# Seven products for eight: the second product onto a copy of the first, and a unit's last two behind the next unit's first

## The chip, the core and the metric

The kernel runs on one core of a Trainium2 chip. The metric is the device time of one execution in microseconds, as the median of several runs. The engines are called by the short names of the profile: PE (TensorE, the matrix engine; PEld is its weight load), DVE (VectorE), ACT (ScalarE), POOL (GpSimd) and SP (SyncE, which issues the DMAs). PE writes only into PSUM, so every product must be copied or added out of PSUM by DVE or ACT. That step is called an eviction here.

## The reference

One inference step of one layer of a streaming encoder with three gated branches, over 1024 prompt tokens and 64 sample tokens, in float32:

```
shift, scale, gate = silu(c) @ W_ada + b_ada
h = rmsnorm(x, pre_g) * (1 + scale) + shift
z = h @ w_in                      # 1024 x 8720, cut into the branches' columns
A: trailing means minus token, per-group linear;  B: spatial gating on chunks of 128
C: gated linear attention with a low-rank decay
y_a, y_b, y_c: each branch * silu(its gate columns)
m = sigmoid(gm_a) * (y_a @ w_oa) + sigmoid(gm_b) * (y_b @ w_ob) + sigmoid(gm_c) * (y_c @ w_oc)
out = m @ w_out
y = x + gate * rmsnorm(out, post_g)
```

Outputs are y for both token sets, the pooling history, the attention state and the normalised rows of branch B.

## The kernel before

Every float32 operand is split into two parts, `hi` and `lo` (function `split`, L359, for activations and `w_split`, L555, for weights), and a product is the sum of hi·hi, hi·lo and lo·hi. The large projections go through `s_unit` (L573). One unit makes 256 output channels for all tokens: the two halves of its channels, the even and odd blocks of 128 input channels, and the two token pieces of 544 (512 prompt and 32 sample) form a 2 x 2 block product, which Winograd's form does with seven products instead of eight. There are 42 units: 34 for w_in, with four input blocks per product (`nkk` = 4, 24 matmuls of 272 columns), four for w_oa with two blocks (12 matmuls) and four for w_oc with four.

A unit holds three PSUM tiles of two banks each: `pA` and `pB`, which it takes in turn from two (`spsum`, L212), and `pC`, the tile `third` (L207). In the profile the first two are called `sps` and the last `third`. The order of one unit (L618 to L663), with what is evicted behind each product:

1. B11 into pA; ACT copies it to `p1`.
2. T2 into pB; DVE: `u2 = p1 + pB`.
3. B21 onto pA; ACT copies it to `c11`, which is finished.
4. T3 onto pB; DVE: `u3 = p1 + pB`.
5. T1 into pC; DVE: `u3 += pC`.
6. T4 onto pB; DVE: `p1 += pB`, finished.
7. B22 onto pC; DVE: `u2 += pC`; `u2` and `u3` are finished.

A product that goes onto a tile must wait for the eviction of what stands there. The names that count for the profile are `u<-p,sps` (steps 2 and 4), `u<-u,third` (steps 5 and 7), `p<-p,sps` (step 6), `p<-sps` (step 1) and `c<-sps` (step 3). Behind a finished tile runs `post`, which differs by unit (a tanh on ACT, a gate, transposes) and ends in a store, issued by `put_later` one step on. In the last two projections `post_m` (L1377) also loads `z_gm` and `z_m` blocks by DMA and adds them.

The first unit of each of the three operands (`feed`, L620 to L627) computes B11, T2 and T1 together, block by block, as its operands are made.

Generators set the program's order. `run` plays units one after the other and `weave` (L1729) plays the steps of a second task between those of units: the decay (L725), nine stretches of the attention (`gla`, `gla_sample`) among 19 units of w_in (L1801, L1814, L1844), the spatial gating, the loads of the next operand. Except at the very start, a planner then sets the order on each engine: it takes the program's order as priority, lets weight loads and weight splits go 400 places ahead (`ahead`), and uses its own estimate of times. On the chip each engine works through its list in that order, and an instruction that waits holds up all behind it on its engine.

The phases are: w_in units (to L1846), the w_oa units (L1874), plain products for w_ob (L1880), the w_oc units (L1893 and L1903), the last product `out_phase` (L1915).

Of the kernel before, what the change touches and what calls it, by code (L numbers as in the profile page):

```python
# [58 lines left out]
class InOrder:  # L59
    """an engine whose instructions, while asked for, keep the order of the program"""  # L60
# [18 lines left out]
def tile_hybrid_pool_sgu_gla_step(  # L79
# [55 lines left out]
    def nm(base):  # L135
        serial[0] += 1
        return f"{base}_{serial[0]}"
# [58 lines left out]
    def role(name, dt=F32):  # L196
        """a tile of the attention; each role has its own slots, so that none waits
        for a tile of another role that comes earlier in the program"""
        return roles[name](name, dt)[:, 0:TH]
# [11 lines left out]

    def spsum():  # L212
        return psum.tile([P, 2, 512], F32, name=nm("sps"), tag="sps", bufs=2)
# [4 lines left out]
    # ------------------------------------------------------------ constants  # L218
# [30 lines left out]
    def condition():  # L249
        """silu of the conditioning rows, as columns"""  # L250
        ps = apsum()
        c = cols[:, 46:62]
        pe.transpose(ps[:, 0:16], crows, ident[0:16, 0:16])
        dve.tensor_copy(c, ps[:, 0:16])
        act.activation(th_c, c, AF.Tanh, scale=0.5)
        dve.scalar_tensor_tensor(ccv, th_c, 1.0, c, op0=ALU.add, op1=ALU.mult)
        dve.tensor_scalar(
            cc[:, :, 0:2], ccv.rearrange("p (s k) -> p k s", s=2), 0.5, None, op0=ALU.mult
        )
        dve.tensor_copy(ccs[:, :, 0:2], cc[:, :, 0:2])  # L260
        dve.tensor_sub(ccs[:, :, 2:4], cc[:, :, 0:2], ccs[:, :, 0:2].bitcast(F32))
        dve.tensor_add(pair, ident[0:4, 0:2], ident[0:4, 2:4])
# [22 lines left out]
    # ------------------------------------------------------------ scratch in DRAM  # L285
# [39 lines left out]
    # ------------------------------------------------------------ x  # L325
# [63 lines left out]
    def x_transpose(k, p):  # L389
        """one half of the prompt, channels on partitions"""  # L390
# [61 lines left out]
    # ------------------------------------------------------------ adaLN  # L452
# [29 lines left out]
    def ada_shift_scale(q):  # L482
        """the shift and the scale of two k blocks"""
# [63 lines left out]
    # ------------------------------------------------------------ products, seven for eight  # L547
# [25 lines left out]
    def s_unit(src, c0, Bb, nkk, post, off=0, raw=None, feed=None):  # L573
        """256 output channels by all tokens; channels on partitions.  The two column
        halves, the even and odd k blocks and the two token pieces are the 2 x 2 blocks
        of the two operands (Winograd's form with seven products)."""
# [41 lines left out]
        pA, pB = spsum(), spsum()  # L618
        vA, vB = pA[:, :, 0:CH], pB[:, :, 0:CH]
        if feed:  # L620
            pC = third
# [5 lines left out]
            feed(nkk)  # L627
        else:
            product(pA, A(0, 0), "B11", True)
        p1 = stage("p1", F32)  # L630
        act.copy(view(p1), vA)
        yield nkk
        if not feed:
            product(pB, s2, "T2", True)
        u2 = stage("u2", F32)
        dve.tensor_add(view(u2), view(p1), vB)
        yield nkk
# [7 lines left out]
        u3 = stage("u3", F32)  # L645
        dve.tensor_add(view(u3), view(p1), vB)
        yield nkk
        if not feed:
            pC = third
            product(pC, s1, "T1", True)  # L650
        vC = pC[:, :, 0:CH]
        dve.tensor_add(view(u3), view(u3), vC)
        yield nkk
        product(pB, A(1, 1), "T4", False)
        dve.tensor_add(view(p1), view(p1), vB)
        post(1, 0, p1)
        yield nkk
        s4 = sf(A(0, 1), s2, True)
        product(pC, s4, "B22", False)
        dve.tensor_add(view(u2), view(u2), vC)  # L660
        post(0, 1, u2)
        post(1, 1, u3)
        yield nkk  # L663

    # ------------------------------------------------------------ constants used later
# [43 lines left out]
    # ------------------------------------------------------------ decay  # L709
# [15 lines left out]
    def decay(din):  # L725
# [3 lines left out]
        for terms in ((("B11", 0),), (("B21", 1),), (("T1", 0), ("B22", 1))):  # L729
            ps = third if len(acc) == 2 else spsum()  # L730
# [14 lines left out]
        d = blk("zd")[0:32, 0:PC]  # L745
        act.copy(halves(d), acc[0])
# [12 lines left out]
        def soft(items):  # L759
            """log sigmoid of each (src, dst, bias): min(x, 0) - ln(1 + exp(-|x|))"""  # L760
# [61 lines left out]
    # ------------------------------------------------------------ first phase: w_in  # L822
# [28 lines left out]
    def silu2(t):  # L851
        """t = 2 * silu(t)"""
        th = blk("th")[:, 0:PC]
        act.activation(th, t, AF.Tanh, scale=0.5)
        dve.scalar_tensor_tensor(t, th, 1.0, t, op0=ALU.add, op1=ALU.mult)
# [203 lines left out]
    # ------------------------------------------------------------ attention  # L1059
# [21 lines left out]
    def level_mask(li, s, L):  # L1081
        """the valid pairs of one level, the same for each of four chunks"""
# [3 lines left out]
    def decayed(q, k, bc, W, L):  # L1086
        """exp of the chunk totals, k scaled to the chunk's end, q scaled from its start"""
# [267 lines left out]
    def w_unit(src, c0, nk, alloc=None):  # L1355
        """hi and lo of 256 columns, as k block -> (hi, lo)"""
# [20 lines left out]
    def post_m(br, u):  # L1377
        """one branch's part of the sum; the last one's blocks go on to the last product"""
# [36 lines left out]
    def plain_units(w, src):  # L1415
        """one branch's part of the sum by plain products, onto what is there"""
# [99 lines left out]
    def wo_load(n, kks=range(4)):  # L1516
        """what is read of w_out for one of the seven products"""
# [7 lines left out]
    def wo_in(n):  # L1525
        """the moving operand of one of the seven products, a k block at a time"""
# [38 lines left out]
    def out_phase(w, sums):  # L1565
# [16 lines left out]
        def final(i, h, t, eng, n=P):  # L1582
            """one half of the columns of a token block"""
# [16 lines left out]
        def finish():  # L1600
            """the rest of the token block that was ready last, behind the next one's product"""
# [17 lines left out]
        def tail(ps, w, odd, first, last):  # L1619
            """hi and lo of the sample rows side by side, so that one product serves both"""  # L1620
# [98 lines left out]
    # ------------------------------------------------------------ order of emission  # L1719
# [9 lines left out]
    def weave(main, side, ratio):  # L1729
        """main, with so much of side in between"""  # L1730
# [10 lines left out]
        run(side)  # L1741

    with first:
# [31 lines left out]
        def feed(j):  # L1775
# [10 lines left out]
        run(s_unit(win, O_Q, Hb, 4, keep(z_q[0:2]), raw=raw, feed=feed))  # L1786
        weave(
            chain(win_unit(O_K, keep(z_k[0:2])), win_unit(O_Q + 256, keep(z_q[2:4]))),
            decay(din),
# [17 lines left out]
        for u in range(2):  # L1807
# [7 lines left out]
            chain(  # L1815
                *(
                    win_unit(o + u * 256, post(u))
                    for u in range(2)
                    for o, post in ((O_U, post_u), (O_GB, post_gb))
# [6 lines left out]
        weave(sgu(), chain(*gm[0:3]), 3.0)  # L1826
# [18 lines left out]
        run(gate_steps)  # L1845
# [20 lines left out]
    def units(w, blocks, nkk, br, us=range(4)):  # L1866
# [8 lines left out]
        units(woa, Ab, 2, 0),  # L1875
# [17 lines left out]
    run(units(woc, Cb, 4, 2, range(3)))  # L1893
# [9 lines left out]
    for n, step in zip(PRODUCTS, zip(units(woc, Cb, 4, 2, (3,)), steps)):  # L1903
# [73 lines left out]
```

## Time and profile before

| | |
|---|---|
| runs (three) | 1338.26, 1342.36, 1343.36 us |
| median | 1342.36 us |
| span of the profiled execution | 1337.9 us |
| busy PE | 92% |
| busy DVE, ACT, POOL | 71%, 42%, 50% |
| DMA | 195.38 MB, mean 146 GB/s |

The profile is of one execution. "Busy" is a share of the span; idle time of PE shows up in the list of PE's waits with the instruction that ended it. The granted clock of PE is given per stretch as a share of the full 2.4 GHz; 0.5 is the lower level of 1.2 GHz.

### The profile page before, as it was taken

The numbers are of one execution on the slowest core, as the hardware profiler recorded it, in microseconds if no ns is written. First come the engines' busy times: TensorE is split into PE (matmuls) and PEld (weight loads), VectorE is DVE, ScalarE is ACT, GpSimd is POOL, SyncE is SP. The second block draws the span as 40 slices with busy tenths as digits, with TensorE's granted clock in tenths as the row PEclk, the third lists the DMA queues.
The fourth block names the chain that finished last, engine by engine and source line by source line (L and its number), as shares of the span: only waits on it lengthen the run. The fifth ranks groups of instructions, "written<-read, shape, count | busy, mean of one in ns | idle before, by whom it ended". The sixth has DMA issues, their size and how long they took to land.

```text
span 1337.9 us, 23855 instructions
## 1 busy us (share of the span) xinstructions
PE 1226.6 (92%) x8962; PEld 1147.0 (86%) x8962; DVE 948.3 (71%) x1458; ACT 562.1 (42%) x1133; POOL 674.5 (50%) x528
## 2 busy tenths in 40 slices
PE   5789899998999998999999999899997998997796
PEld 3289799997989998999998999899987898996674
DVE  6975844556675788786468757876459789779957
ACT  7636533353534324345333345355354333233533
POOL 4652344333443546463347445253337498568625
PEclk9889899998999999999999999999998998999898
DMA  8512523232423213232235535445456799667065
GB/s 284 162 58 72 193 82 108 88 121 74 139 74 113 68 52 117 70 118 73 76 102 197 166 109 163 146 142 153 118 164 213 257 343 337 201 203 267 19 198 198
DMA packets 144609, 195.38 MB, mean 146 GB/s; under 512 B 18505, under 2 KB 82047, under 8 KB 144494
## 3 DMA queue, kind: packets, MB, share of 16 engines
q1 hardware_dynamic: 144494, 193.86, 44.5%
q8 instruction: 70, 1.15, 0.3%
q14 instruction: 45, 0.37, 0.1%
HBM read 133.59 MB, written 60.22 MB: 145 GB/s over the span
## 4 chain that ended last, share of the span: by engine, by line
PE 45%; DVE 13%; DMA 6%; issue 4%; POOL 3%; ACT 1%; SPq 0%; DVEq 0%; POOLq 0%; ACTq 0%
PE sps L70 27%; PE third L70 11%; PE aps L70 7%; DVE x L70 4%; DVE h L70 3%; DMA h<-z_m 1%; DVE u L70 1%; DMA late<-in_ada_w_dram 1%; DVE lo L70 1%; DVE late L70 1%; POOL sf L70 1%; DMA x<-z_yc 1%; DVE p L70 1%; POOL x L70 1%; DMA x<-z_bc 1%
## 5 line engine op out<-in xcount | busy, mean ns | idle before, releaser
L70 PE MATMUL sps<-h,hi 128*128 128x272 f32 x3344 | 589.1, 296 | 19.1 <-ACT x L70 6.9
L70 PEld LDWEIGHTS sps<-h,hi 128*128 128x128 f32 x3344 | 486.9, 193 | 27.9 <-ACT x L70 7.7
L70 PE MATMUL sps<-h,lo 128*128 128x272 f32 x1672 | 358.8, 295 | 2.1 <-DVE lo L70 1.9
L70 PEld LDWEIGHTS sps<-h,lo 128*128 128x128 f32 x1672 | 269.5, 192 | 5.6 <-DVE lo L70 2.8
L70 PE MATMUL third<-h,hi 128*128 128x272 f32 x1344 | 237.0, 294 | 12.4 <-DVE u L70 8.3
L70 PEld LDWEIGHTS third<-h,hi 128*128 128x128 f32 x1344 | 193.7, 190 | 16.4 <-DVE u L70 5.0
L70 ACT CAST hi<-sf 128x512 fp32r<-128x512 f32 (+1 forms) x168 | 100.3, 598 | 196.5 <-PE sps L70 160.5
L70 PE MATMUL third<-h,lo 128*128 128x272 f32 x672 | 144.3, 294 | 0.6 <-POOL lo L70 0.6
L70 ACT CAST hi<-raw 128x512 fp32r<-128x512 f32 (+1 forms) x134 | 80.1, 598 | 139.2 <-PE third L70 69.6
L70 POOL TENSOR_TENSOR lo<-sf,hi 128x512 fp32r<-128x512 f32 (+1 forms) x57 | 77.5, 1360 | 96.7 <-ACT hi L70 68.4
L70 DVE TENSOR_TENSOR lo<-sf,hi 128x512 fp32r<-128x512 f32 (+1 forms) x111 | 90.9, 819 | 42.7 <-ACT hi L70 35.7
L70 POOL TENSOR_TENSOR sf<-raw,raw 128x512 f32<-128x512 f32 (+1 forms) x38 | 50.1, 1319 | 140.3 <-DMA raw<-in_w_in_dram 71.6
L70 POOL TENSOR_TENSOR lo<-raw,hi 128x512 fp32r<-128x512 f32 (+1 forms) x45 | 61.0, 1357 | 100.6 <-ACT hi L70 88.1
L70 DVE TENSOR_TENSOR x<-x 128x256 f32<-128x256 f32 (+6 forms) x142 | 95.9, 707 | 22.2 <-DMA x<-z_bc 8.2
L70 PEld LDWEIGHTS third<-h,lo 128*128 128x128 f32 x672 | 106.8, 189 | 3.5 <-issue 1.7
L70 POOL TENSOR_TENSOR x<-x,x 128x256 f32<-128x256 f32 (+2 forms) x71 | 73.2, 1041 | 71.1 <-ACT x L70 52.4
L70 DVE TENSOR_TENSOR u<-p,sps 128x544 f32<-128x544 f32 x84 | 60.2, 717 | 63.1 <-PE sps L70 55.4
L70 ACT ACTIVATE x<-x 128x512 f32<-128x512 f32 (+2 forms) x104 | 57.9, 567 | 105.1 <-DVE x L70 96.3
L70 DVE TENSOR_TENSOR lo<-raw,hi 128x512 fp32r<-128x512 f32 (+1 forms) x89 | 77.0, 865 | 34.3 <-ACT hi L70 23.6
L70 DVE TENSOR_TENSOR u<-u,third 128x544 f32<-128x544 f32 x84 | 60.1, 716 | 47.5 <-PE third L70 47.3
L70 POOL TENSOR_TENSOR sf<-raw,sf 128x512 f32<-128x512 f32 (+1 forms) x38 | 51.5, 1356 | 78.2 <-DVE lo L70 77.4
L70 DVE TENSOR_TENSOR x<-x,x 128x256 f32<-128x256 f32 (+4 forms) x100 | 71.1, 723 | 12.9 <-ACT x L70 12.3
(290 smaller groups left out, 1918.3 us busy)
## 6 DMA issues: line engine op xcount, KB each, us to landing
raw<-in_w_in_dram SPq DMA_DIRECT2D x68, 512.0 KB, 3.9
x<-z_gm SPq DMA_DIRECT2D x48, 272.0 KB, 4.8
x<-z_m SPq DMA_DIRECT2D x32, 272.0 KB, 5.4
h<-z_m SPq DMA_DIRECT2D x28, 272.0 KB, 5.0
h<-in_x_prompt_dram SPq DMA_DIRECT2D x28, 256.0 KB, 6.1
z_gm<-u SPq DMA_DIRECT2D x24, 272.0 KB, 2.2
h<-in_ada_w_dram SPq DMA_DIRECT2D x24, 256.0 KB, 4.7
x<-z_yc SPq DMA_DIRECT2D x16, 272.0 KB, 5.1
```

Source lines behind the costliest of these rows:

```text
L70: return f(*args, **kw)
```

## The change

PSUM tiles pA and pB become two fixed tiles. In a unit, B11 no longer goes out to SBUF: ACT copies pA into pB, and T2 accumulates there onto it, so that every later product on pB already holds B11. The unit's T4 and B22 are put into a generator `rest`, kept in `unfinished`, and issued by the next unit right behind its B11. Where no unit follows, `finish_unit` issues them. The new order is B11, (T4, B22 of the unit before), T2, T1, B21, T3. The evictions are:

- ACT: `pB = pA` after B11; `u` from pB after T2; `c22` from pC after T1; `c11` from pA after B21; `c21` from pB after T4
- DVE: `c22 += pB` after T3; `u += pC` after B22

The first unit of an operand keeps B11, T2 and T1 together: ACT copies `p1`, DVE adds `u = p1 + pB`, ACT copies `u` back into pB.

```diff
+    pair_ps = [psum.tile([P, 2, 512], F32, name=f"sps{i}", tag=f"sps{i}", bufs=1) for i in range(2)]
     def spsum():
-        return psum.tile([P, 2, 512], F32, name=nm("sps"), tag="sps", bufs=2)
+        pair_turn[0] += 1
+        return pair_ps[1 - pair_turn[0] % 2]
...
-        pA, pB = spsum(), spsum()
+        (pA, pB), pC = pair_ps, third
...
         if feed:
...
+            p1 = stage("p1", F32)
+            act.copy(view(p1), vA)
+            yield nkk
+            dve.tensor_add(view(u), view(p1), vB)
+            act.copy(vB, view(u))
+            act.copy(view(c22), vC)
...
         else:
             product(pA, A(0, 0), "B11", True)
-        p1 = stage("p1", F32)
-        act.copy(view(p1), vA)
-        yield nkk
-        if not feed:
-            product(pB, s2, "T2", True)
-        u2 = stage("u2", F32)
-        dve.tensor_add(view(u2), view(p1), vB)
+            yield nkk
+            yield from finish_unit()
+            act.copy(vB, vA)
+            product(pB, s2, "T2", False)
+            act.copy(view(u), vB)
+            yield nkk
+            product(pC, s1, "T1", True)
+            act.copy(view(c22), vC)
             yield nkk
         product(pA, A(0, 1), "B21", False)
         c11 = stage("c11", F32)
         act.copy(view(c11), vA)
...
         product(pB, s3, "T3", False)
-        u3 = stage("u3", F32)
-        dve.tensor_add(view(u3), view(p1), vB)
-        yield nkk
-        if not feed:
-            pC = third
-            product(pC, s1, "T1", True)
-        vC = pC[:, :, 0:CH]
-        dve.tensor_add(view(u3), view(u3), vC)
-        yield nkk
-        product(pB, A(1, 1), "T4", False)
-        dve.tensor_add(view(p1), view(p1), vB)
-        post(1, 0, p1)
+        dve.tensor_add(view(c22), view(c22), vB)
         yield nkk
         s4 = sf(A(0, 1), s2, True)
-        product(pC, s4, "B22", False)
-        dve.tensor_add(view(u2), view(u2), vC)
-        post(0, 1, u2)
-        post(1, 1, u3)
-        yield nkk
+        def rest():
+            product(pB, A(1, 1), "T4", False)
+            c21 = stage("c21", F32)
+            act.copy(view(c21), vB)
+            post(1, 0, c21)
+            yield nkk
+            product(pC, s4, "B22", False)
+            dve.tensor_add(view(u), view(u), vC)
+            post(0, 1, u)
+            post(1, 1, c22)
+            yield nkk
+        unfinished.append((rest(), blk_now))
...
 -            ps = third if len(acc) == 2 else spsum()
+            ps = (*pair_ps, third)[len(acc)]
...
+            if len(acc) == 1:
+                d = blk("zd")[0:32, 0:PC]
+                act.copy(halves(d), acc[0])
+                yield 2.0
...
         run(s_unit(win, O_Q, Hb, 4, keep(z_q[0:2]), raw=raw, feed=feed))
+        low = decay(din)
+        next(low)
+        run(finish_unit())
+        next(low)
...
-        run(gate_steps)
+        run(gate_steps, finish_unit())
...
-        units(woa, Ab, 2, 0),
+        chain(units(woa, Ab, 2, 0), finish_unit()),
...
-    run(units(woc, Cb, 4, 2, range(3)))
+    run(units(woc, Cb, 4, 2, range(3)), finish_unit())
...
+    whole = chain(units(woc, Cb, 4, 2, (3,)), finish_unit())
+    for n, step in zip(("B11", "T2", "T1", "B21", "T3", "T4", "B22"), zip(whole, steps)):
```

Before two of the weaves `entered` plays the first three steps of the first unit, so that the unit before is complete when the second task begins.

## Rows read from the trace of the kernel before

**Rows 1.** Page, part 1: busy time, share and count by engine.

```profile
PE 1226.6 (92%) x8962; PEld 1147.0 (86%) x8962; DVE 948.3 (71%) x1458; ACT 562.1 (42%) x1133; POOL 674.5 (50%) x528
```

**Rows 2.** Busy time by stretch: length, PE, PEld, DVE, ACT, POOL, granted clock, DMA.

```profile
300.00:400.00 100.00, 89.43 (x711) 86.37 (x710) 67.00 (x107) 40.39 (x86) 42.89 (x35) 0.95 0.30 94
...
600.00:700.00 100.00, 100.00 (x803) 99.40 (x802) 61.22 (x116) 38.96 (x89) 39.92 (x34) 1.00 0.25 79
...
1000.00:1100.00 100.00, 90.29 (x682) 88.13 (x681) 84.27 (x101) 40.12 (x80) 69.36 (x55) 0.97 0.80 268
```

**Rows 3.** Waits of PE: who waited for whom, total us, times, longest.

```profile
PE third L70 <- DVE u L70: 10.0, 5, 4.0
PE sps L70 <- ACT x L70: 6.9, 2, 3.7
PE sps L70 <- DVE u L70: 6.1, 7, 2.4
PE sps L70 <- DVE p L70: 2.3, 2, 1.6
...
PE sps L70 <- ACT c L70: 0.8, 1, 0.8
```

**Rows 4.** Timeline of PE: start, duration, instructions, idle before and releaser.

```profile
715.38 0.41 PE L70 MATMUL third<-h,lo 128*128 128x272 f32 x2
...
720.14 0.82 PE L70 MATMUL sps<-h,hi 128*128 128x272 f32 x4 [3.24 <-ACT x L70]
...
1028.42 0.77 PE L70 MATMUL sps<-h,hi 128*128 128x272 f32 x4 [0.76 <-ACT c L70]
```

**Rows 5.** Timeline of DVE ahead of the stall at 720 us.

```profile
712.83 6.54 DVE L70 TENSOR_TENSOR x<-x 128x512 f32<-128x512 f32 x7
719.29 0.71 DVE L70 TENSOR_TENSOR u<-p,sps 128x544 f32<-128x544 f32 x1
```

**Rows 6.** Busy time by stretch around six of PE's stalls, columns as in rows 2.

```profile
154.00:161.00 7.00, 5.84 (x26) 5.87 (x27) 4.88 (x13) 4.52 (x13) 3.77 (x3) 0.51 0.61 213
310.00:316.00 6.00, 3.23 (x15) 2.88 (x15) 5.16 (x7) 1.66 (x4) 3.31 (x4) 0.59 0.21 53
378.00:387.00 9.00, 8.33 (x58) 8.13 (x57) 6.72 (x12) 2.33 (x5) 2.44 (x3) 0.81 0.20 62
...
719.00:728.00 9.00, 7.86 (x51) 7.89 (x52) 8.37 (x13) 3.33 (x6) 7.78 (x7) 0.81 0.23 72
...
1017.00:1025.00 8.00, 5.17 (x25) 5.20 (x26) 7.67 (x10) 3.67 (x9) 5.57 (x4) 0.57 0.79 253
1028.00:1032.00 4.00, 3.58 (x28) 3.58 (x29) 2.90 (x6) 1.45 (x4) 3.92 (x4) 1.00 0.83 261
```

**Rows 7.** Groups of evictions: count, busy us, mean ns, idle before, what ended it.

```profile
L70 DVE TENSOR_TENSOR u<-p,sps 128x544 f32<-128x544 f32 x84 | 60.2, 717 | 63.1 <-PE sps L70 55.4 <-ACT p L70 5.4 <-DMA z_yb<-t 1.4
L70 DVE TENSOR_TENSOR u<-u,third 128x544 f32<-128x544 f32 x84 | 60.1, 716 | 47.5 <-PE third L70 47.3
...
L70 DVE TENSOR_TENSOR p<-p,sps 128x544 f32<-128x544 f32 x42 | 30.0, 715 | 19.2 <-PE sps L70 19.0
...
L70 ACT COPY p<-sps 128x544 f32<-128x544 f32 x42 | 25.5, 608 | 1.9 <-PE sps L70 1.9
L70 ACT COPY c<-sps 128x544 f32<-128x544 f32 x42 | 25.5, 606 | 0.1
```

**Rows 8.** Chain that ended last: start, us, engine and tile; one whole product.

```profile
594.78 3.02 PE third L70 x24
```

**Rows 9.** Timeline of ACT: a copy, the cast behind it, and another copy.

```profile
1017.84 0.60 ACT L70 COPY p<-sps 128x544 f32<-128x544 f32 x1
1018.34 0.64 ACT L70 CAST h<-T 128x544 fp32r<-128x544 f32 x1
...
1027.76 0.61 ACT L70 COPY c<-sps 128x544 f32<-128x544 f32 x1
```

**Rows 10.** Waits of ACT, same columns as rows 3.

```profile
ACT x L70 <- DVE x L70: 109.3, 66, 4.4
```

More of the change, by code (lines that the diff above doesn't have):

```diff
@@ L210, in apsum @@
         return psum.tile([P, 512], F32, name=nm("aps"), tag="aps", bufs=2)
+    pair_ps = [psum.tile([P, 2, 512], F32, name=f"sps{i}", tag=f"sps{i}", bufs=1) for i in range(2)]
+    pair_turn = [0]
     def spsum():
-        return psum.tile([P, 2, 512], F32, name=nm("sps"), tag="sps", bufs=2)
+        pair_turn[0] += 1
+        return pair_ps[1 - pair_turn[0] % 2]
     def halves(ap):
@@ L616, in view @@
             return halves(t[:, off : off + PC])
-        pA, pB = spsum(), spsum()
-        vA, vB = pA[:, :, 0:CH], pB[:, :, 0:CH]
+        (pA, pB), pC = pair_ps, third
+        vA, vB, vC = (x[:, :, 0:CH] for x in (pA, pB, pC))
+        u, c22 = stage("u", F32), stage("c22", F32)
+        blk_now = cur["blk"]
         if feed:
-            pC = third
+            assert not unfinished
             ws = [w_split(w, nkk) for w in (A(0, 0), s2, s1)]
@@ L627, in s_unit @@
             feed(nkk)
+            p1 = stage("p1", F32)
[6 more added lines that the diff above has]
+            yield nkk
         else:
             product(pA, A(0, 0), "B11", True)
-        p1 = stage("p1", F32)
-        act.copy(view(p1), vA)
-        yield nkk
-        if not feed:
-            product(pB, s2, "T2", True)
-        u2 = stage("u2", F32)
-        dve.tensor_add(view(u2), view(p1), vB)
-        yield nkk
+            yield nkk
[6 more added lines that the diff above has]
+            act.copy(view(c22), vC)
+            yield nkk
         product(pA, A(0, 1), "B21", False)
@@ L644, in s_unit, with finish_unit @@
         product(pB, s3, "T3", False)
-        u3 = stage("u3", F32)
-        dve.tensor_add(view(u3), view(p1), vB)
-        yield nkk
-        if not feed:
-            pC = third
-            product(pC, s1, "T1", True)
-        vC = pC[:, :, 0:CH]
-        dve.tensor_add(view(u3), view(u3), vC)
-        yield nkk
-        product(pB, A(1, 1), "T4", False)
-        dve.tensor_add(view(p1), view(p1), vB)
-        post(1, 0, p1)
+        dve.tensor_add(view(c22), view(c22), vB)
         yield nkk
         s4 = sf(A(0, 1), s2, True)
-        product(pC, s4, "B22", False)
-        dve.tensor_add(view(u2), view(u2), vC)
-        post(0, 1, u2)
-        post(1, 1, u3)
-        yield nkk
+        def rest():
[3 more added lines that the diff above has]
+            post(1, 0, c21)
+            yield nkk
+            product(pC, s4, "B22", False)
+            dve.tensor_add(view(u), view(u), vC)
+            post(0, 1, u)
+            post(1, 1, c22)
+            yield nkk
+        unfinished.append((rest(), blk_now))
+    unfinished = []
+    def finish_unit():
+        while unfinished:
+            g, own = unfinished.pop()
+            for _ in range(2):
+                now, cur["blk"] = cur["blk"], own
+                c = next(g)
+                cur["blk"] = now
+                yield c
     lc = {}
@@ L729, in decay @@
         for terms in ((("B11", 0),), (("B21", 1),), (("T1", 0), ("B22", 1))):
-            ps = third if len(acc) == 2 else spsum()
+            ps = (*pair_ps, third)[len(acc)]
             n = 0
@@ L744, in decay @@
             acc.append(ps[0:32, :, 0:CH])
-        d = blk("zd")[0:32, 0:PC]
-        act.copy(halves(d), acc[0])
+            if len(acc) == 1:
+                d = blk("zd")[0:32, 0:PC]
+                act.copy(halves(d), acc[0])
+                yield 2.0
         z3 = []
@@ L1741, in weave, with entered @@
         run(side)
+    def entered(g):
+        for _ in range(3):
+            next(g)
+            tick()
+        return g
     with first:
@@ L1786, in tile_hybrid_pool_sgu_gla_step @@
         run(s_unit(win, O_Q, Hb, 4, keep(z_q[0:2]), raw=raw, feed=feed))
+        low = decay(din)
+        next(low)
+        run(finish_unit())
+        next(low)
         weave(
             chain(win_unit(O_K, keep(z_k[0:2])), win_unit(O_Q + 256, keep(z_q[2:4]))),
-            decay(din),
+            low,
             1.0,
@@ L1814, in tile_hybrid_pool_sgu_gla_step @@
         weave(
[L1815 to L1819, printed above, removed]
+            entered(
+                chain(
+                    *(
+                        win_unit(o + u * 256, post(u))
+                        for u in range(2)
+                        for o, post in ((O_U, post_u), (O_GB, post_gb))
+                    )
                 )
@@ L1825, in tile_hybrid_pool_sgu_gla_step @@
         run(win_unit(O_VB, post_vb(0)), win_unit(O_VB + 256, post_vb(1)))
-        weave(sgu(), chain(*gm[0:3]), 3.0)
+        weave(sgu(), entered(chain(*gm[0:3])), 3.0)
         roles["X"] = ring(ROLES["X"])
@@ L1902, in tile_hybrid_pool_sgu_gla_step @@
     )
-    for n, step in zip(PRODUCTS, zip(units(woc, Cb, 4, 2, (3,)), steps)):
+    whole = chain(units(woc, Cb, 4, 2, (3,)), finish_unit())
+    for n, step in zip(("B11", "T2", "T1", "B21", "T3", "T4", "B22"), zip(whole, steps)):
         give(*((slot, i) for i in places[n]))
```

## Prediction

> **What bounds the kernel now.** I read the busy shares first. PE is busy for 1226.6 of 1337.9 us and DVE for 948.3, so PE is the bound and DVE the next in line [rows 1]. The stretches show where PE is not full: between 600 and 700 us it is busy without a gap at the full clock and gets through 803 matmuls, while between 300 and 400 and between 1000 and 1100 it is idle for about 10 us each and gets through 711 and 682 [rows 2]. So a gain can only come from PE's idle time and from what follows it.
>
> The list of PE's waits says what ended that idle time [rows 3]. Five waits of a product on `third` and nine on `sps` ended with a DVE eviction, 10.0, 6.1 and 2.3 us. The two waits of 6.9 us put down to an ACT instruction belong there too. At 720.14 PE starts 3.24 us late [rows 4], and on DVE the eviction `u<-p,sps` ended 0.14 us before it, at 720.00 [rows 5]; the other wait, of 3.7 us, has the same form, at 155 us. Together DVE evictions held PE up for 10.0 + 6.1 + 2.3 + 6.9 = 25.3 us. Evictions on ACT held it up for 0.8 us [rows 3].
>
> Why DVE is late is seen at the same place: the product that served as cover ended at 715.8 us, but seven attention operations stood in DVE's queue from 712.83 us, for 6.54 us, ahead of the eviction [rows 4, 5]. By its place behind a product on `sps` and ahead of a T1 it is step 4, `u3`, for which T4 waits. It took 0.71 us itself; the lateness is the queue's.
>
> A stall costs more than its idle time where the granted clock falls behind it. Around the 3.24 us at 720 the clock was 0.81 over 9 us, a loss of 9 x 0.19 = 1.7 us; the stretches from 747 and from 866 us, behind stalls of 1.6 and 2.2 us, show the same 0.81. At 154, 310, 378 and 1017 it was 0.51 over 7, 0.59 over 6, 0.81 over 9 and 0.57 over 8 us: 3.4, 2.5, 1.7 and 3.4 us [rows 6]. In the stretches from 310 and 378 waits for attention operations stand beside the evictions, so I count half. The clock share of DVE's evictions is 3.4 + 1.25 + 0.85 + 3 x 1.7 + 3.4 = 14.0 us. So 25.3 + 14.0 = 39.3 us hang on DVE evictions.
>
> **The change part by part.** *Evictions.* A unit had five on DVE and two on ACT; now it has two on DVE and five on ACT, and three on DVE in the three first units. DVE loses 42 x 3 - 3 = 123 adds of 0.716 us, 88 us of its 948 (9%); ACT gains 126 copies of 0.607 us, 76 us on 562 [rows 1, 7]. None of this is on PE's path by itself; it counts by who waits. PE's own work stays the same: the same matmuls on the same operands. The copy from PSUM to PSUM has no row; I bound it by the 0.61 us of the copy to SBUF from above and half of it from below, and take 0.61, the nearest row.
>
> *What each product waits for.* A product with four input blocks lasts 3.0 us [rows 8], one with two half of that. Before, T3, T4 and B22 wait for a DVE add with one product in between as cover, T2 for one with two, and B21 for an ACT copy with one. Now T4 waits for DVE (`c22`) with the next unit's B11 as cover and T1 for DVE (`u += pC`) with T2 as cover. B11 waits for the ACT copy `c11` behind T3, T3 for an ACT copy with two products as cover, and B22's tile was emptied four products before. So three DVE gates of one product become two, and the T2 gate leaves DVE. If the remaining gates are as late as the old ones, a third goes: 39.3 / 3 = 13.1 us. Of the 26.2 left, the 9% lighter queue saves about 2.5. Bounds: by exact gates only T3's and T2's share would go, at the least the 2.3 us of `p<-p,sps`; at most all 39.3.
>
> *The new gate.* T2 now waits for two ACT copies in a row: `c21` out of pB after the last unit's T4, then pA into pB. B22, 3.0 us, is the cover. On ACT a copy is followed by the next instruction 0.50 us after its start, and PE started 0.05 us after a copy's end (1027.76 + 0.61 = 1028.37, 1028.42) [rows 4, 9]. With one weight cast ahead of them the copies are done after 0.1 + 0.5 + 0.5 + 0.61 + 0.05 = 1.76 us, 1.25 us before B22 ends. In the three later w_oa units, where B22 lasts 1.5 us, they are 0.25 us late: 0.75 us. In the three first units, T3 waits for one ACT copy more, behind B21: up to 0.6 us each, 1.8. I take 2 us for both (0 to 2.6). Behind the waiting copy on ACT stand the weight casts of the following products and the posts; PE has two products' weights in hand then, so 1.25 us more don't reach it.
>
> *Phase ends.* Where no unit follows, T4 stands directly behind T3, with the DVE add between them bare: after w_in, after w_oa, after the third and the fourth w_oc unit. The first unit has the decay's first group there. Each costs at least 0.05 + 0.72 + 0.05 = 0.8 us, and with the queue of these stretches up to the longest wait of 4.0 us [rows 3]; where the planner finds products of the next phase to put there, nothing. I take 1.25 each, 5 us (0 to 16).
>
> *Moved with T4 and B22.* Their posts, stores and, in w_oa and w_oc, the loads of `z_gm` and `z_m` on SP's queue come a product later, behind the next unit's weight load, which went 400 places ahead anyway. What reads them is a phase away, except in the last w_oc unit, whose T4 and B22 stay sixth and seventh. I cost this at nothing; the next unit's B11 hides it. The tiles of the stage ring live about as long as before (`p1`, `u2`, `u3` before; `u`, `c22` now). The decay's groups keep their three tiles and evictions; nothing.
>
> *Sum.* 13.1 + 2.5 - 2 - 5 = 8.6 us less: 1329.3 against the profiled span of 1337.9. That span lies 4.5 us below the median of 1342.4 and 0.4 below the fastest of the three runs. Against the median it is 1333.8, and I say 1334.
>
> **The rivals.** *Nothing to see, about 1341.* The planner makes a new list for every engine. The remaining DVE gates may meet the attention's queue as often as before, since T4, which waited at 720, still waits for a DVE add; then the gain is the 2.3 us, and the phase ends take it. For it speaks that lateness came from single queues [rows 5]; against it the lighter DVE.
>
> *Not what it says, about 1341.* The planner may already put the next unit's B11 ahead of a late T4, as it orders by its estimate; then the new order adds no cover and only the move from DVE to ACT counts.
>
> *Nearly all goes, 1310.* If the lighter queue lets the two remaining DVE gates be met, 39.3 - 7 = 32 us. Against it: the 6.54 us of attention ahead of one eviction stay in the queue.
>
> *Slower, 1358.* The two copies stand behind an ACT instruction that itself waits. ACT's attention operations waited 66 times for DVE, 1.7 us in the mean, at the longest 4.4 [rows 10]. T2's gate has 1.25 us to spare. If in half of the 19 units with attention between them a wait of 3 us stands there, 9.5 x (3 - 1.25 + 0.85 for the clock in every second) = 25 us are lost, 16 more than the gain. It decides from about 9 us of stalls at T2. Against it: copies on ACT have held PE up for only 0.8 us so far, and their groups waited for hardly anything but PE [rows 3, 7].
>
> *Clock lost in every unit, 1400.* If T2 came a little late in each of the 39 units that follow another and the clock fell each time, 39 x 1.7 = 66 us would be added to 1334. Behind the 0.76 us at 1028 the clock stayed at 1.00 [rows 4, 6], which speaks against it. The Trainium skill (TensorE: Matmul & The Clock Gate, "A second HAM failure mode: psum-queue depth-cycling") tells of a kernel whose cycling through PSUM let PE idle briefly between groups until its clock swung between both levels; by that rule this rival is the outcome, by the row small gaps cost only themselves.
>
> **How the numbers follow.** Forecast 0.50 (1326 to 1340), nothing to see 0.20, not what it says 0.05, nearly all 0.10, slower 0.12, clock 0.03. Half a percent, 6.7 us, is about what a measurement here can tell from no change: faster is under 1335.6, slower over 1349.1. Faster: 0.40 of the forecast's 0.50 and 0.10, together 0.50. Same: 0.10, 0.17 and 0.05, 0.32. Slower: 0.03 of the second, 0.12 and 0.03, 0.18. The range 1314 to 1352 leaves out most of "nearly all", most of "slower" and the clock case, about 0.17.
>
> **What would show it.** DVE's busy time near 860 us and ACT's near 638. In PE's waits, DVE evictions down from 25.3 to about 16 us and hardly any wait of `sps` for ACT copies; the granted clock higher in the attention stretches. Wrong if waits of `sps` for ACT copies add up to over 9 us, if the phase ends open gaps of several microseconds, or if DVE evictions still hold PE up for 25 us.

## The result, and the profile after

The changed kernel took 1359.86 us in the median (1357.60 to 1361.57), the kernel before 1341.41 us on the same chip: a ratio of 1.014, 95% interval 1.0117 to 1.0163. The forecast was 1334, and its range ended at 1352. The profiled execution spans 1356.6 us.

Page of after, part 1, columns as in [rows 1]:

```profile
PE 1221.3 (90%) x8962; PEld 1142.6 (84%) x8962; DVE 870.5 (64%) x1335; ACT 622.9 (46%) x1259; POOL 667.6 (49%) x528
```

PE has 5 us less busy time, DVE 78 less and ACT 61 more. PE's idle time made the difference. The stretches of [rows 2] after, with two more:

```profile
300.00:400.00 100.00, 95.72 (x781) 91.74 (x780) 61.92 (x102) 47.93 (x106) 42.21 (x37) 1.00 0.29 91
600.00:700.00 100.00, 99.82 (x801) 99.14 (x800) 51.63 (x106) 45.31 (x102) 41.81 (x37) 1.00 0.26 84
700.00:800.00 100.00, 89.06 (x690) 87.17 (x688) 63.23 (x95) 38.82 (x73) 47.57 (x37) 0.95 0.47 150
...
1000.00:1100.00 100.00, 86.05 (x650) 84.14 (x649) 69.45 (x86) 47.82 (x94) 59.89 (x50) 0.95 0.71 232
```

From 300 to 400 us PE gets through 781 matmuls instead of 711, as hoped. From 1000 to 1100 it does 650 instead of 682. From 700 to 800 it does 690, where before did 749:

```profile
700.00:800.00 100.00, 94.89 (x749) 93.81 (x748) 73.08 (x112) 36.41 (x64) 55.65 (x44) 0.97 0.48 158
```

PE's waits of after that answer to [rows 3]:

```profile
PE sps L70 <- ACT sps L70: 20.7, 11, 7.7
...
PE sps L70 <- ACT c L70: 9.0, 3, 7.3
PE sps L70 <- DVE c L70: 7.3, 4, 4.0
PE third L70 <- DVE u L70: 6.9, 3, 4.2
```

DVE evictions hold PE up for 7.3 + 6.9 = 14.2 us, down from 25.3. In their place stand the copies on ACT: 20.7 us for a copy into pB (16.8 of them for the copy of pA, which T2 waits for, and 3.9 for the copy of `u` in the first units of w_oa and w_oc, which T3 waits for), and 9.0 us behind copies to `c11` or `c21`, of which 7.3 us is one wait of the last product. That makes 29.7 us where before had 0.8. One of the longest, on ACT and then on PE:

```profile
783.49 0.62 ACT L70 CAST x<-x 128x512 fp32r<-128x512 f32 x1 [1.75 <-DVE x L70]
784.01 0.61 ACT L70 CAST hi<-sf 128x512 fp32r<-128x512 f32 x1
784.53 0.60 ACT L70 COPY c<-sps 128x544 f32<-128x544 f32 x1
785.16 0.66 ACT L70 ACTIVATE c<-c 128x544 f32<-128x544 f32 x1
785.73 0.61 ACT L70 COPY sps<-sps 128x544 f32<-128x544 f32 x1
...
786.39 1.28 PE L70 MATMUL sps<-h,hi 128*128 128x272 f32 x4 [3.42 <-ACT sps L70]
```

An attention cast waits for DVE, then come a weight cast, `c21`, the tanh of the post behind it, and only then the copy for T2. Ahead of the last product `c21` stands behind operand casts of the next phase, which wait 5.4 us for DVE:

```profile
1235.16 1.47 ACT L70 CAST h<-h 128x544 fp32r<-128x544 f32 x3 [5.39 <-DVE h L70]
1237.58 0.65 ACT L70 CAST h<-h 128x544 fp32r<-128x544 f32 x1 [0.95 <-DVE h L70]
1238.13 0.61 ACT L70 COPY c<-sps 128x544 f32<-128x544 f32 x1
...
1238.79 1.65 PE L70 MATMUL sps<-x,h 128*128 128x512 f32 x3 [7.29 <-ACT c L70]
```

One more thing has grown, which at first sight has nothing to do with evictions. Waits of ACT, of POOL and of SP's queue for the weights, in before and then in after (`raw`: the weights as loaded; `sf`: POOL's sums of them; `hi` and `lo`: the two halves of a weight block, `hi` cast by ACT):

```profile
ACT hi L70 <- POOL sf L70: 21.1, 9, 4.3
...
POOL sf L70 <- DMA raw<-in_w_in_dram: 71.6, 17, 10.5
...
SPq L70 <- DVE lo L70: 225.1, 46, 22.8
SPq L70 <- POOL lo L70: 97.1, 21, 14.8
...
SPq L70 <- POOL sf L70: 30.2, 20, 3.8
```

```profile
ACT hi L70 <- POOL sf L70: 93.6, 31, 8.5
...
POOL sf L70 <- DMA raw<-in_w_in_dram: 134.4, 27, 11.2
...
SPq L70 <- DVE lo L70: 186.8, 25, 22.7
SPq L70 <- POOL sf L70: 158.7, 34, 9.7
...
SPq L70 <- POOL lo L70: 40.3, 14, 17.2
```

SP's queue, which waits until a weight tile has been read, doesn't wait much longer in all (352.4 and 385.8 us): the wait for POOL's sums is five times as long, those for `lo` are shorter. But the loads themselves come later. Counted in PE's matmuls, from the timelines of SP's queue and PE, the load of a w_in unit's second weight tile is issued 20 matmuls later than before (the median of units 2 to 33; a product has 24). POOL waits longer for the loads, and ACT stands for 93.6 us in front of casts whose operand isn't there. Evictions in ACT's queue stand behind them.

### The profile page after: what moved, and what is told of

Read it like the earlier page. It is cut to its first block, busy times and chain, and to the rows that moved or that the text cites. A ratio compares the mean times of both kernels' runs of the same rounds, so it can differ in the third digit from the quotient of the medians.

```text
span 1356.6 us, 23821 instructions
## 1 busy us (share of the span) xinstructions
PE 1221.3 (90%) x8962; PEld 1142.6 (84%) x8962; DVE 870.5 (64%) x1335; ACT 622.9 (46%) x1259; POOL 667.6 (49%) x528
## 5 line engine op out<-in xcount | busy, mean ns | idle before, releaser
L70 PE MATMUL sps<-h,hi 128*128 128x272 f32 x3344 | 592.7, 297 | 42.4 <-ACT sps L70 20.7
L70 DVE TENSOR_TENSOR lo<-sf,hi 128x512 fp32r<-128x512 f32 (+1 forms) x111 | 95.9, 865 | 110.5 <-ACT hi L70 106.0
L70 DVE TENSOR_TENSOR x<-x 128x256 f32<-128x256 f32 (+6 forms) x142 | 90.5, 670 | 46.9 <-DMA x<-z_bc 21.5
L70 DVE TENSOR_TENSOR h<-h,h 128x544 fp32r<-128x544 f32 (+4 forms) x47 | 51.6, 1123 | 12.9 <-DMA h<-in_w_out_dram 7.3
L70 PE MATMUL aps<-x,x 128*128 128x256 f32 (+6 forms) x352 | 53.5, 287 | 4.1 <-ACT x L70 2.0
```

What stands on the lines that cost most here:

```text
L70: return f(*args, **kw)
```

## The experiments

All kernels run the same 8962 matmuls, so PE's time can be set against its own progress. The table gives the microseconds between the ends of the matmuls with these numbers, from the timelines of PE (units differ a little in order; w_in ends near 7200, w_oa near 7540, so the row to 7700 holds the end of w_in, w_oa and the start of w_ob, and is called the w_oa stretch below):

| matmuls | before | after | all_old | unit_seed | proj_late | late_noload | first12 |
|---|---|---|---|---|---|---|---|
| to 1000 | 192.4 | 196.9 | 192.7 | 190.3 | 195.1 | 189.3 | 189.2 |
| to 2000 | 132.0 | 123.0 | 132.4 | 122.4 | 131.4 | 122.9 | 124.8 |
| to 5000 | 387.9 | 387.0 | 387.4 | 391.9 | 389.2 | 390.6 | 383.9 |
| to 7000 | 267.7 | 279.5 | 265.2 | 267.8 | 265.5 | 263.8 | 265.1 |
| to 7700 | 103.7 | 107.8 | 104.8 | 110.2 | 121.8 | 104.4 | 103.0 |
| to the end | 238.3 | 246.8 | 240.8 | 241.8 | 248.0 | 239.3 | 240.7 |

Ratios below are to the kernel before on the same chip in the same job, with the 95% interval.

**Is it ACT's queue, the chain of two copies, or the late order?** Four variants:

```diff
 seed_on_dve:  -act.copy(vB, vA)          +dve.tensor_copy(vB, vA)
 both_on_dve:  the same, and -act.copy(view(c21), vB)  +dve.tensor_copy(view(c21), vB)
 copies_ahead: both copies inside "with ahead():", 400 places up
 late_only:    deferral kept, no seeding: p1 = copy of pA on ACT; on DVE u = p1 + pB,
               c22 = p1 + pC, c22 += pB, p1 += pB (c21), u += pC
```

> The changed kernel with the copy of pA into pB on DVE; the copy c21 ahead of it stays on ACT. Theory 'ACT queue': only half of the gate leaves ACT, c21 still stands in its list, and the second copy now stands in DVE's; T2's waits stay between 12 and 22 us, 1350 to 1360. Theory 'chain': nothing changes, 1355 to 1362. Theory 'late order': the same, 1355 to 1362.

> The changed kernel with c21 and the copy of pA into pB both on DVE, so that T2's gate doesn't touch ACT. Theory 'ACT queue': if ACT's list is the cause, T2's waits fall under 10 us and the 7.3 us wait of the last product for c21 goes, 1340 to 1350; if every list is as bad, they stay. Theory 'chain': two in a row stay two in a row, T2's waits stay near 20 us, 1355 to 1362. Theory 'late order': 1355 to 1362.

> The changed kernel with c21 and the copy of pA into pB, still on ACT, allowed to go as far ahead in the planner's list as the weight casts. Theory 'ACT queue': they pass the attention operations, T2's waits fall from 20.7 to under 12 us, and the 7.3 us at the last product shrink, 1343 to 1352. Theory 'chain': the two copies take the same 1.2 us, T2's waits stay, 1355 to 1362. Theory 'late order': 1355 to 1362.

> The late T4 and B22 alone: T2 starts its tile fresh as before, B11 goes out to p1 on ACT, and the five other evictions are adds on DVE (u = p1 + pB, c22 = p1 + pC, c22 += pB, p1 += pB, u += pC). Theory 'ACT queue' (the loss is that the two copies for which T2 waits stand in ACT's list behind attention operations and casts that themselves wait): PE has no wait of sps for ACT sps, the 20.7 us of these waits and the clock behind them go, 1335 to 1345. Theory 'chain' (two evictions in a row are too long for one product's cover): the same, 1335 to 1345, since T2 waits for one add. Theory 'late order' (bare phase ends and later posts cost, whatever engine evicts): 1355 to 1362 as in the changed kernel.

Measured: seed_on_dve 1366.32 us, 1.0216 (1.0192 to 1.0239); both_on_dve 1372.04 us, 1.0249 (1.0228 to 1.0271); copies_ahead 1357.17 us, 1.0151 (1.0129 to 1.0173); late_only 1354.99 us, 1.0134 (1.0116 to 1.0152). The copies are no better off on DVE (PE waited 21.5 us for the one copy there, 24.5 us with both), and a better place in ACT's list, with 16.3 us of waits, changes nothing in the time that can be measured. Deferral without any seeding costs as much as the whole change. There DVE's eviction of T4 is what T2 waits for, in PE's waits of late_only (2.3 us in [rows 3]):

```profile
PE sps L70 <- DVE p L70: 24.1, 7, 7.6
```

So whichever engine evicts, the eviction behind the deferred T4 is late. "ACT queue" falls as the net cause; "late order" stands.

**Seeding without deferral.** unit_seed keeps the copies and the fixed tiles, with all seven products inside the unit; unit_plain has the same order on the kernel before, unseeded.

```diff
-B11, (T4, B22 of the unit before), T2, T1, B21, T3
+B11, T1, T2, B21, T3, B22, T4
```

> Seeds as the changed kernel does (ACT copies pA into pB, five of the seven evictions on ACT), but defers nothing: the order inside the unit is B11, T1, T2, B21, T3, B22, T4, so that T1 covers the copy, B22 the add behind T3, and T4's copy has the next unit's B11 and T1 to be done in. Whole computation. Theory 'late order' (the loss comes from T4 and B22 being issued a product later and from the cover that this takes from T2, whatever engine evicts): no loss is left, 1328 to 1343 us beside about 1338 for the kernel before, PE's waits of sps for ACT copies under 8 us (29.7 in the changed kernel), and no gap of several us behind the decay near 170 us and in front of the last product near 1235 us. Theory 'ACT queue' (the loss comes from evictions standing behind ACT instructions that wait for DVE): the copies are as late as before, by up to 5 us in a tenth of the units against a cover of 3.0 us, 15 us or more of such waits, and 1350 to 1362 us.

> The same order inside the unit (B11, T1, T2, B21, T3, B22, T4) on the kernel before: no seeding, no deferral, two evictions on ACT and five on DVE as before. Whole computation. It tells what the seeding alone is worth, by unit_seed less this one. 'Late order': 1333 to 1343 us, DVE busy near 948 us; if the seeding is a gain by itself, this one is 3 to 10 us above unit_seed. 'ACT queue': this one is at 1338 and unit_seed 12 to 24 us above it.

Measured: unit_seed 1346.19 us, 1.0068 (1.0045 to 1.0091); unit_plain 1360.10 us, 1.0154 (1.0127 to 1.0181). Half of the change's loss goes with the deferral. The waits of unit_seed that are left for ACT's copies:

```profile
PE sps L70 <- ACT sps L70: 4.9, 4, 1.6
```

4.9 us instead of 20.7. Against unit_plain the seeding is worth 14 us. Evictions have little part in that: they held PE up for 15.7 us in unit_plain and 12.9 in unit_seed. And unit_plain came out 17 us above the highest figure expected of it: its order alone costs 1.5%, and PE's waits show it waiting for weights:

```profile
PE sps L70 <- ACT hi L70: 10.2, 5, 5.3
...
PE sps L70 <- DVE lo L70: 9.6, 4, 3.6
```

All waits of PE for the halves `hi` and `lo` of a weight block add up to 27.3 us there, 13.8 in unit_seed and 8.2 in before.

**Where is it lost?** One kernel in which each unit's form can be chosen by its number (`old`: unseeded, in before's order; `unit`: as in unit_seed; `late`: as in the change) made the next six:

```diff
 woven_in_place: unit for 0-3, 6-11, 16-19, 22-33 (beside a second task), late elsewhere
 ends_in_place:  unit for 0, 33, 37, 40, 41 (no next unit), late elsewhere
 win_unit:       unit in w_in (0-33), old in w_oa and w_oc
 win_late:       late in w_in, old in w_oa and w_oc
 proj_late:      old in w_in, late in w_oa and w_oc
 all_old:        old everywhere
```

> The changed kernel, but units that share the time with a second task (decay, attention, gating: units 0 to 3, 6 to 11, 16 to 19, 22 to 33) finish T4 and B22 themselves, in the order of unit_seed; deferral is left in units 4, 5, 12 to 15, 20, 21 and in the last two projections. Whole computation. Beside about 1338 before, 1357 for the changed kernel and 1346 for unit_seed. Theory 'cover' (deferral takes T2's two ACT copies from a cover of two products to one, and that costs where a second task's instructions that wait stand ahead of them): the stalls at 171, 758 and 786 us go, 1344 to 1351 us. Theory 'phase ends' (deferral costs where no next unit follows): 1352 to 1358 us, since four of the five phase ends are left.

> The changed kernel, but only the units with no next unit behind them (0, 33, 37, 40 and 41: the first, and the last of w_in, of w_oa, and the third and fourth of w_oc) finish T4 and B22 themselves, in the order of unit_seed; all others defer. Whole computation. 'Phase ends': the 7.3 us in front of the last product and the 7.7 us at 171 us go, 1344 to 1350 us. 'Cover': the stalls at T2 in the middle of the phases stay, 1351 to 1357 us.

> No deferral anywhere: the 34 w_in units as in unit_seed (seeded, B11, T1, T2, B21, T3, B22, T4), the eight units of the last two projections unseeded in the order of the kernel before. Whole computation. unit_seed was some 9 us ahead of the kernel before at the end of w_in (a unit's time set against the same unit's) and gave it back in the last two projections. If that comes from the order there (T1 early, the sums of its operands needed sooner), 1326 to 1335 us, below the kernel before; if it comes with an earlier arrival at a phase that waits for its loads, 1338 to 1346 us.

> The changed kernel in w_in (seeded and deferred, units 0 to 33), the last two projections unseeded and not deferred, in the order of the kernel before. Whole computation. In the trace of the changed kernel PE is about 6 us behind the kernel before at the end of w_in and 19 us at its own end. If the two parts add up by place: 1344 to 1350 us beside about 1340 for the kernel before. If the last projections' loss is only what w_in hands on: 1354 to 1360 us.

> The reverse: w_in unseeded and not deferred, in the order of the kernel before; the last two projections as in the changed kernel. Whole computation. By place: 1349 to 1356 us (the 12 to 13 us that the changed kernel loses behind w_in). If the loss is made in w_in: 1337 to 1343 us.

> What is left of the change without its two parts: the two fixed PSUM tiles and the decay's first group taken out of the weave; every unit unseeded, undeferred, in the order of the kernel before. Whole computation. A control for the others: 1336 to 1343 us if these details and the new plan cost nothing; 1346 us or more if they are part of the loss.

Measured: woven_in_place 1358.83 us, 1.0143 (1.0122 to 1.0164); ends_in_place 1353.87, 1.0091 (1.0059 to 1.0124); win_unit 1340.88, 1.0003 (0.9989 to 1.0017); win_late 1351.44, 1.0084 (1.0057 to 1.0110); proj_late 1364.48, 1.0178 (1.0159 to 1.0197); all_old 1341.34, 1.0023 (1.0008 to 1.0037). Neither "cover" nor "phase ends" comes out: undoing the deferral beside second tasks gave nothing back, at the phase ends a third. Nor does the loss add up by place: above all_old w_in alone costs 0.6%, the projections alone 1.5%, both together about 1.2%. The details that come along (all_old) cost 0.2%.

proj_late is the key, since its w_oa stretch took 121.8 us instead of 104.8. Timelines of POOL, SP's queue, POOL again, ACT and PE there:

```profile
1047.24 1.34 POOL L70 TENSOR_TENSOR h<-x,h 128x544 fp32r<-128x544 f32 x1 [5.51 <-ACT h L70]
1048.53 1.23 POOL L70 TENSOR_TENSOR lo<-raw,hi 128x256 fp32r<-128x256 f32 x1
...
1049.79 0.38 SPq L70 DMA_DIRECT2D raw<-in_w_oa_dram  x1
...
1055.06 0.72 POOL L70 TENSOR_TENSOR sf<-raw,raw 128x256 f32<-128x256 f32 x1 [5.30 <-DMA raw<-in_w_oa_dram]
...
1056.62 0.71 ACT L70 CAST hi<-sf 128x256 fp32r<-128x256 f32 x2 [3.41 <-POOL sf L70]
...
1057.07 0.77 PE L70 MATMUL sps<-h,hi 128*128 128x272 f32 x4 [4.26 <-ACT hi L70]
```

POOL's part of T4's split ends at 1049.76 us, behind an instruction that waited 5.51 us for ACT. The load into the tile is issued at 1049.79, the sum starts at 1055.06, the cast at 1056.62, and PE has stood still for 4.26 us. The code says why the load is late: there are two tiles of raw weights (`NRAW` = 2) and a unit takes both. T4's operand A(1, 1) is a block of the second, read as it was loaded, so the tile is free only when T4's weights are split. They are split at most three products ahead (`NW` = 3). Before, T4, B22 and B11 ran between the start of T4 and T2, whose operand needs the new tile; deferred, T4 and B22. In unit_seed and unit_plain it is T4 and B11 ahead of T1. So all the new orders give the next unit's load, its sums and its casts one product less.

**Weights or cover?** Taking the loads away (78 of the 84 loads of these weights are left out, so the results are not the layer's), and giving w_oa a second buffer:

```diff
 old_noload (from all_old) and late_noload (from the changed kernel):
-    raw = w_raw(src, c0, nkk)
+    if key not in loaded:            # key: w_in, w_oa or w_oc
+        loaded[key] = w_raw(src, c0, nkk)
+    raw = loaded[key]
 proj_late_1raw, first12_1raw and after_1raw, w_oa only:
-    r = a raw tile for each half
+    r = one raw tile; the halves are r[:, 0:2, :] and r[:, 2:4, :]
```

> all_old (every unit unseeded and undeferred, in the order of the kernel before) with the weights of the seven-product units loaded once for each of the three operands: all 34 w_in units use the first unit's weights, the four w_oa and the four w_oc units those of their first. Left out: the loads of the other units' weights, 78 of 84; sums, splits and products stay. No tile of raw weights is then waited for or given back. It is the base for late_noload: 1325 to 1342 us, since weights held PE up little in the kernel before.

> The changed kernel with the same loads left out. With loads the changed kernel stands some 16 us above all_old. Theory 'weights' (T4 and B22 keep the unit's raw weights and sums a product longer; the next unit's load, its sums on POOL and ACT's cast of them come later, and ACT's evictions stand behind that cast): without loads the distance to old_noload is 6 us or less, ACT's waits of hi for POOL's sf fall from 93.6 us to under 40. Theory 'cover' (T2 waits for two ACT copies with one product as cover, whatever the weights do): the distance stays 12 to 19 us.

> proj_late (w_in in the order of the kernel before, the last two projections as in the changed kernel) with both halves of a w_oa unit's weights in one tile of raw weights, of which a w_oa unit fills only half: the next unit's load no longer waits until this unit's weights are split. Whole computation. In proj_late the w_oa stretch (PE's matmuls 7000 to 7700) took 122 us against 105 in all_old, and POOL's sums waited 17.0 us for w_oa loads against 0.9. 'Weights': 8 us or more of the 17 come back, 1347 to 1357 us beside 1364 for proj_late. 'Cover': 1360 to 1368 us.

Measured: old_noload 1341.68 us, 1.0020 (1.0002 to 1.0037), which is all_old's time: loads by themselves cost nothing there. late_noload 1329.71 us, 0.9940 (0.9915 to 0.9965). With loads the change stands 16 us above all_old (1.0140 against 1.0023, of 1341), without them 12.0 us below old_noload. By the table, leaving out the loads takes back what the change lost in each stretch: 196.9 becomes 189.3 us, 279.5 becomes 263.8, 107.8 becomes 104.4 and 246.8 becomes 239.3. Part 1 of old_noload's page and of late_noload's, then two of PE's waits and one of ACT's in late_noload; POOL's waits for w_in loads are gone:

```profile
PE 1223.0 (91%) x8962; PEld 1145.0 (86%) x8962; DVE 945.9 (71%) x1458; ACT 562.8 (42%) x1133; POOL 666.8 (50%) x528
...
PE 1214.9 (92%) x8962; PEld 1135.2 (86%) x8962; DVE 882.2 (67%) x1335; ACT 626.1 (47%) x1259; POOL 672.2 (51%) x528
...
PE sps L70 <- ACT c L70: 12.3, 5, 6.9
...
PE sps L70 <- ACT sps L70: 8.8, 7, 2.2
...
ACT hi L70 <- POOL sf L70: 4.6, 2, 2.4
```

ACT's wait for sums fell from 93.6 to 4.6 us and PE's for copies into pB from 20.7 to 8.8. What makes late_noload faster than old_noload is not the evictions, though: they held PE up for 23.8 us in old_noload and 27.2 in late_noload. Its waits for `hi` and `lo` fell from 13.6 to 1.6 us, and the same matmuls took 8.1 us less, at a mean granted clock of 0.975 where old_noload had 0.965. proj_late_1raw took 1351.84 us, 1.0094 (1.0063 to 1.0126): 0.8% or some 11 us less than proj_late, from this one edit. The stretch from 1000 to 1100 us in proj_late, proj_late_1raw and all_old:

```profile
1000.00:1100.00 100.00, 78.02 (x538) 75.30 (x537) 61.41 (x77) 41.65 (x84) 50.45 (x44) 0.90 0.62 202
```

```profile
1000.00:1100.00 100.00, 89.97 (x680) 88.28 (x679) 79.18 (x90) 46.58 (x92) 68.29 (x52) 0.95 0.77 264
```

```profile
1000.00:1100.00 100.00, 88.89 (x666) 86.36 (x664) 85.18 (x102) 38.72 (x77) 69.25 (x54) 0.97 0.80 268
```

538, 680 and 666 matmuls: the second buffer gives back the whole loss of w_oa, with the deferral in place (the w_oa stretch took 104.0 us). This settles "weights" for that stretch. What is left of the loss lies behind it: to the end proj_late_1raw took 250.5 us, all_old 240.8. The Trainium skill (Trainium Kernel Development and Optimization, "Best Practices") says to double-buffer so that loads and computing overlap; these two runs agree, and show that two tiles of which a unit takes both are one buffer.

> The changed kernel itself with both halves of a w_oa unit's weights in one tile of raw weights, nothing else changed. Whole computation. In proj_late this edit took back the whole loss of the w_oa stretch; in the changed kernel POOL's sums waited 3.4 us for w_oa loads, and the stretch lost 4 us on the kernel before. 'Weights': 2 to 6 us back, 1351 to 1357 us beside 1357 to 1360; the loss in w_in and w_oc stays, since no second buffer fits there. If the price is not made in this stretch: 1357 to 1361 us.

Measured: 1356.95 us, 1.0121 (1.0085 to 1.0157), no difference to the changed kernel that can be told. Its w_oa stretch became 1.3 us shorter (106.5 from 107.8). It lost little there to begin with. In w_in and w_oc a unit fills both tiles, and a second buffer was not tried there.

**A gain in one stretch.** first12 uses `unit` in units 0 to 11 and `old` behind; first12_1raw has w_oa's one tile too.

> Seeded without deferral (B11, T1, T2, B21, T3, B22, T4) in units 0 to 11 alone, where unit_seed gained some 10 us on the kernel before; all other units in the form of the kernel before. Whole computation. If a gain is kept where nothing behind it changes: 1327 to 1334 us. If later work that waits for other engines takes it back: 1337 to 1343 us.

> first12 (seeded without deferral in units 0 to 11, the rest as the kernel before), with the same one tile for a w_oa unit's weights. Whole computation. In first12 POOL's sums waited 2.4 us for w_oa loads: little is to be had, 1320 to 1327 us beside 1325.

Measured: first12 1324.84 us, 0.9894 (0.9879 to 0.9909): faster than both kernels. first12_1raw 1326.42 us, 0.9911 (0.9883 to 0.9940), the same. The stretch that lost 10 us to idle time in [rows 2], in first12:

```profile
300.00:400.00 100.00, 97.14 (x797) 93.87 (x796) 60.67 (x101) 47.63 (x103) 44.92 (x37) 1.00 0.34 104
```

797 matmuls instead of 711, and what is won stays won: behind unit 11 the parts of the table stay within 4 us of before's. Why twelve units in this form gain 1.1% and all 34 of w_in (win_unit) nothing is not shown.

## Why the prediction was wrong, point by point

*What each product waits for: right for DVE, and the gain is luck.* DVE evictions were to hold PE up for about 16 us, and it was 14.2; DVE was to be busy for about 860 us and ACT for 638, and it was 870.5 and 622.9. But the sum counted on fewer waits for evictions in all, and these did not come: with the copies on ACT they went from 26.1 us to 43.9, and to 27.2 in late_noload. The change gains 12 us without loads, and the seeding 14 between unit_plain and unit_seed, which is near the 8.6 of the sum; but in both pairs it was PE's waits for the weight halves that fell, by 12.0 and 13.5 us, and the prediction has no term for them. Why they fell is not shown.

*Moved with T4 and B22: this is the step that failed.* It followed their posts, stores and loads and cost them at nothing, since "the next unit's weight load [...] went 400 places ahead anyway". It asked what the moved products issue and not what they hold. A load's place in the list is worth nothing while the tile that it fills is still to be read, and the deferred T4 is that tile's last reader. The two runs without loads put the price at 28 us: 16 above all_old with loads, 12 below old_noload without. That is the price for the whole change; no run without loads parts the deferral from the seeding.

*The new gate: mis-sized.* I took 2 us (0 to 2.6), from an ACT row in which a copy followed the instruction before it without a wait [rows 9]. It became 20.7 us, or 8.8 without loads. With the copies to `c11`, `c21` and `c22`, which I cost at nothing, PE waited 29.7 us for ACT's copies, or 21.9 without loads, far over the 9 us that I had named as a sign of being wrong. A timing from a prompt stretch said nothing of the attention stretches: at 783 us the copy had four instructions ahead of it, the first of which came late itself.

*Phase ends: about as sized.* I took 5 us (0 to 16), and undoing the five ends gave back 0.5%, some 7 us (give or take 5). In the first unit T4 stood for 3.96 us, for `c22` on DVE. The stall of T2 behind it, at 171 us, is 7.67 where before had 3.7 (it is part of the 20.7), and the one for `c21` ahead of the last product 7.29, where before had 4.17 for a load of w_out.

*The rivals.* "Slower, 1358" had the time almost exactly and half of the mechanism: T2's copies did stand behind ACT instructions that wait for DVE, as at 783 us. But ACT's waits of `x` for DVE did not grow (102.9 us against 109.3 in [rows 10]), and moving the copies off ACT made it worse, so ACT's queue alone is not the cause. "Nothing to see" is out by the stretch from 300 to 400, where PE got through 70 matmuls more. "Not what it says" is not put out by it, since first12, which defers nothing, does more there still; its 1341 us are out. "Clock lost in every unit" did not come: from 600 to 700 us T2 took its turn on a tile behind two copies in each unit, and yet PE was busy for 99.82 us of 100 and the clock stayed at 1.00. The brief idling of which the Trainium skill (TensorE: Matmul & The Clock Gate, "A second HAM failure mode: psum-queue depth-cycling") tells did not arise there, so that these runs do not test its rule.

*What stays open.* For w_oa the way from a late load to a late product is in the trace. In w_in it is only shown that the loads come later and that the loss goes with them. The wait that grew in SP's queue there is the one for POOL's sums, the last readers of the first tile; T4 holds only the second. The casts that wait for sums stand directly ahead of few late copies: in after's timeline of ACT, evictions whose product was done stood for 41 us, summed over all 204, behind attention operations `x<-x` that waited, and for 11 us behind a waiting `hi<-sf`. In late_noload the first sum is 25 us and the second nothing. And each kernel is planned anew, so its list changes along with its waits: the same `late` units cost 17 us in w_oa behind one w_in and 3 to 4 behind the other. How much of w_in's part runs through the waiting casts and how much through the list is not settled.

## What to carry to other kernels

When a step is moved later, ask what it is the last reader of: every buffer it holds delays the load, and all that is made from the load, by up to as much as the step moved. Take a wait's price from the stretch in which it will stand, not from the cleanest row. And try a part of a change in one stretch before the whole: here the seeding without the deferral, in twelve units, gained 1.1% where the whole change lost 1.4%.

## What the runs showed of the hardware

A stall was paid twice in proj_late. Behind the 4.26 us gap at 1057 us the clock dropped to its lower level for some 3 us (the granted clock was 0.59 over the stretch from 1058 to 1062); a group of four matmuls took 1.11 us where the same group took 0.67 at 1051:

```profile
1051.89 0.67 PE L70 MATMUL third<-h,hi 128*128 128x272 f32 x4
...
1058.45 1.11 PE L70 MATMUL sps<-h,hi 128*128 128x272 f32 x4
```

A copy from PSUM into PSUM on ACT, for which no row of before had a price, took 0.61 us at 785.73 us and 0.608 in the mean of the 39, the same as one to SBUF [rows 7].
